# Weight splits skewed by a step between ScalarE and VectorE, and result banks handled one by one, in a two-layer decoder trunk on one core

## The chip, the cores and the metric

The kernel runs on 1 core of one Trainium2 chip. The metric is device time in microseconds (us) of one execution. The kernel before takes 1994.87 us (median of 3 runs, 1994.66 to 1995.28). In the traces the engines are named PE (TensorE, the matrix products), PEld (its weight loads), DVE (VectorE), ACT (ScalarE), POOL (GpSimdE) and SP (SyncE, which issues the DMA transfers).

## The reference

256 positions of 2048 channels go through two layers. Each layer adds to x a token mixer, a cross-attention to a memory of 256 positions, and a gated FFN, each behind an RMS norm. Only the structure matters here:

```python
def swiglu(h, w_in, w_out):
    g, u = jnp.split(h @ w_in, 2, axis=-1)
    return (jax.nn.silu(g) * u) @ w_out

for i in range(DEPTH):                       # DEPTH = 2
    h = rms_norm(x, norm_mix[i])
    if i % 2 == 0:
        x = x + pool_mixer(h, pool_w[ia], pool_scale[ia])
    else:
        x = x + dsa_attention(h, attn_w_in[ib], attn_w_out[ib], cos_a, sin_a, cos_i, sin_i)
    x = x + memory_cross_attention(rms_norm(x, norm_xattn[i]), memn,
                                   xattn_w_q[i], xattn_w_kv[i], xattn_w_o[i])
    x = x + swiglu(rms_norm(x, norm_ffn[i]), ffn_w_in[i], ffn_w_out[i])
return rms_norm(x, norm_final)
```

Everything is in float32. The FFN's hidden width is 5632; its weights are most of the 368 MB that are read.

## The kernel before

x stays in SBUF. The weights come once from HBM, as **pieces** of 128 x 2048 float32, in the order in which they are used. SP issues a transfer (L157, `load_to`) into one of three buffers named `raw`. Each piece is then **split** into two fp32r tiles: the high part, a copy on ScalarE (`high`, L167, tile `wh`), and the low part, raw minus high, on VectorE (`low`, L170, tile `wl`). The activations are split in the same way. A product of float32 accuracy is three products of fp32r, xh·wh, xh·wl and xl·wh: L413 to L415 outside the FFN (L438, L439 in the transposed form), L759 to L761 in the FFN (`three`). One such product is 128 x 128 by 128 x 512.

Some pieces of the FFN are of another kind, called "seven" here: they enter a scheme of seven instead of eight block products. Their split makes `bh`, `bl` from the piece itself, sums on VectorE within the piece (L200, L202, L203), and `th`, `tl` from the sums. Their left sides are the `sums` tiles: differences of blocks of the activations (`combine`, L402 to L405 on VectorE), which are split like the rest, the high by ScalarE, the low by VectorE.

The order of all instructions is that in which the Python code writes them; every engine takes its own in this order. The code of the products calls `hook` after each small group of them (in the FFN six products). `hook` runs a due job, a piece of side work, and one or two steps of the split of a coming piece (`split_unit`). A step of a plain piece is one half: high and low of 1024 columns. How far ahead the split may run is limited by the number of `w` tiles held: at most 8 exist, and `state["cap"]` limits the hooks to 6 (`W_SHORT`) or 8 (`W_BUFS`). Before the last use `w_get` does what is still missing. `split_unit` also calls for the load of the piece three ahead.

The cross-attention ends with the output product: four column blocks n of 512. After each, `done` adds the two banks to x (`add_to_x`, L506 on VectorE), and starts the next norm's work on that block: a square on ScalarE (L336), transposes on TensorE (L386), their high on ScalarE (L377), their low on VectorE (L379), and for the sums a scaled copy on ScalarE (L393).

The FFN runs over groups of hidden blocks, (0,4), (4,8), (8,11). `chunk_in` (22 calls in the kernel) multiplies 8 pieces into four banks; then VectorE adds the other parts of the result (L852), ScalarE takes Silu (L854), VectorE multiplies (L855). `chunk_out` (two halves n per group) multiplies the gated blocks by the second weights into four banks, and adds to x in the middle (`mid`, L895 to L902) and at the end (L912). `blocks` holds the products of both; it returns after the last of them, so that the code behind the loop handles the four banks in a row. There are four banks for such results, so that the next `blocks` needs the first of them at its first product.

## Time and profile before

| | |
|---|---|
| median of 3 runs | 1994.87 us (1994.66 to 1995.28) |
| profiled execution, its own time | 1993.54 us |
| its span | 1991.7 us |
| TensorE busy | 1953.1 us, 98% of the span |
| VectorE busy | 1554.7 us, 78% |
| ScalarE busy | 1024.1 us, 51% |
| transfers by SP's queue | 370.52 MB, 50.3% of 16 engines' span |
| mean granted TensorE clock | 0.994 of 2.4 GHz |

The terms of the sum come from one profiled execution. Its own time is 1.84 us more than its span and 1.33 us below the median. In time the kernel goes: start, memory keys and values and the first mixer to about 96 us; cross-attention to 192.75; the first FFN to 917; the sparse attention to 1206; cross-attention to 1257; the second FFN to 1981; final norm and output.

A row of a timeline gives the start and the length of an instruction, and in brackets how long the engine stood idle before it and which instruction released it. Rows that follow directly can be grouped, with a count. The products are pipelined: one shows some 0.39 us, but the next starts before it ends.

### The profile page before, as it was taken

How to read it: one execution, taken by the hardware profiler on the slowest of the kernel's cores; microseconds unless marked ns; L12 is line 12 of the kernel's file. 1: busy time of each engine (PE TensorE's matmuls, PEld its weight loads, DVE VectorE, ACT ScalarE, POOL GpSimd, SP SyncE). 2: the span in 40 equal slices, each digit the busy share in tenths (PEclk: the TensorE clock that was granted, in tenths of full speed). 3: DMA queues.
4: the chain of work that ended last, by engine and by line, in shares of the span. 5: the costliest groups of instructions: out<-in, count | busy, mean ns of one | idle time of the engine just before them, and what ended most of it. 6: DMA issues, size and time to landing. Idle time of an engine off the chain costs nothing.

```text
span 1991.7 us, 23621 instructions
## 1 busy us (share of the span) xinstructions
PE 1953.1 (98%) x8986; PEld 1617.5 (81%) x8986; DVE 1554.7 (78%) x2229; ACT 1024.1 (51%) x1462; POOL 29.0 (1%) x73
## 2 busy tenths in 40 slices
PE   9999999999999999999999999899999999999997
PEld 7887788888888888888788888688888888888886
DVE  7865778888888788897687665778878788887897
ACT  6655545455455544555445554655544455544553
POOL 0100000000000000001000000000000000000000
PEclk9999999999999999999999999999999999999999
DMA  9444544545554545545444453455545555544552
GB/s 375 168 150 169 189 171 170 210 186 218 204 195 169 204 177 212 210 169 174 178 149 148 148 193 125 153 208 210 211 169 190 190 192 217 204 191 182 187 204 105
DMA packets 53682, 372.08 MB, mean 187 GB/s; under 512 B 6336, under 2 KB 6976, under 8 KB 9536
## 3 DMA queue, kind: packets, MB, share of 16 engines
q1 hardware_dynamic: 53424, 370.52, 50.3%
q8 instruction: 70, 1.15, 0.2%
q14 instruction: 44, 0.36, 0.1%
q10 hardware_dynamic: 144, 0.05, 0.0%
HBM read 368.45 MB, written 2.10 MB: 186 GB/s over the span
## 4 chain that ended last, share of the span: by engine, by line
PE 91%; DVE 5%; ACT 2%; DMA 1%; issue 1%; SPq 0%; ACTq 0%; DVEq 0%
PE acc L759 19%; PE acc L761 19%; PE acc L760 19%; PE acc L415 5%; PE acc L413 5%; PE acc L414 5%; DVE wl L170 2%; PE acc L438 2%; PE sm L761 1%; PE tp L761 1%; PE tp L760 1%; PE sm L760 1%; PE sm L759 1%; PE tp L759 1%; PE acc L439 1%; DMA raw<-in_xk 1%
## 5 line engine op out<-in xcount | busy, mean ns | idle before, releaser
L170 DVE TENSOR_TENSOR wl<-raw,wh 128x1024 fp32r<-128x1024 f32 (+2 forms) x566 | 665.2, 1213 | 140.7 <-ACT wh L167 138.2
L167 ACT ACTIVATE wh<-raw 128x1024 fp32r<-128x1024 f32 (+2 forms) x566 | 567.1, 1045 | 261.4 <-PE acc L760 96.3
L759 PE MATMUL acc<-wh,big 128*128 128x512 f32 x1616 | 636.5, 394 | 18.5 <-DVE x L506 12.3
L761 PE MATMUL acc<-wh,big 128*128 128x512 f32 x1616 | 630.9, 390 | 0.0
L760 PE MATMUL acc<-wl,big 128*128 128x512 f32 x1616 | 630.6, 390 | 0.0
L759 PEld LDWEIGHTS acc<-wh,big 128*128 128x128 f32 x1616 | 304.5, 188 | 84.4 <-DVE x L506 13.2
L761 PEld LDWEIGHTS acc<-wh,big 128*128 128x128 f32 x1616 | 304.3, 188 | 63.8
L760 PEld LDWEIGHTS acc<-wl,big 128*128 128x128 f32 x1616 | 304.7, 189 | 61.8
L167 ACT ACTIVATE th<-raw 128x1024 fp32r<-128x1024 f32 x186 | 132.4, 766 | 168.7 <-DVE raw L200 129.6
L413 PE MATMUL acc<-wh,big 128*128 128x512 f32 (+1 forms) x480 | 200.6, 418 | 0.0
L415 PE MATMUL acc<-wh,big 128*128 128x512 f32 (+1 forms) x480 | 185.7, 387 | 0.0
L414 PE MATMUL acc<-wl,big 128*128 128x512 f32 (+1 forms) x480 | 184.9, 385 | 0.0
L170 DVE TENSOR_TENSOR bl<-raw,bh 128x1024 fp32r<-128x1024 f32 x124 | 113.1, 954 | 74.9 <-ACT bh L167 74.6
L167 ACT ACTIVATE bh<-raw 128x1024 fp32r<-128x1024 f32 x124 | 98.0, 838 | 128.7 <-issue 79.3
L170 DVE TENSOR_TENSOR tl<-raw,th 128x1024 fp32r<-128x1024 f32 x186 | 151.3, 863 | 5.6 <-ACT th L167 5.6
L415 PEld LDWEIGHTS acc<-wh,big 128*128 128x128 f32 x480 | 90.0, 188 | 18.7
L414 PEld LDWEIGHTS acc<-wl,big 128*128 128x128 f32 x480 | 90.6, 189 | 16.6 <-issue 1.9
L413 PEld LDWEIGHTS acc<-wh,big 128*128 128x128 f32 x480 | 90.3, 188 | 16.4 <-issue 1.9
L438 PE MATMUL acc<-big,wh 128*128 128x512 f32 x256 | 97.0, 417 | 3.2 <-DVE big L379 2.4
L371 DVE TENSOR_TENSOR big<-tp,big 128x512 fp32r<-128x512 f32 x44 | 30.4, 691 | 59.3 <-ACT big L370 59.3
L200 DVE TENSOR_TENSOR raw<-raw 128x1024 f32<-128x1024 f32 x62 | 75.5, 1218 | 0.0
L439 PE MATMUL acc<-big,wl 128*128 128x256 f32 x256 | 72.6, 283 | 1.0 <-DVE wl L170 1.0
(212 smaller groups left out, 2056.5 us busy)
## 6 DMA issues: line engine op xcount, KB each, us to landing
raw<-in_fi SPq DMA_DIRECT2D x176, 1024.0 KB, 4.8
raw<-in_fo SPq DMA_DIRECT2D x88, 1024.0 KB, 4.8
raw<-in_wq SPq DMA_DIRECT2D x16, 1024.0 KB, 4.9
raw<-in_wao SPq DMA_DIRECT2D x16, 1024.0 KB, 4.9
raw<-in_xv SPq DMA_DIRECT2D x8, 1024.0 KB, 6.0
raw<-in_xq SPq DMA_DIRECT2D x8, 1024.0 KB, 4.8
raw<-in_xo SPq DMA_DIRECT2D x8, 1024.0 KB, 4.8
raw<-in_wqi SPq DMA_DIRECT2D x8, 1024.0 KB, 4.9
```

What stands on the lines that cost most here:

```text
L167: A.activation(dst, src, AF.Copy)
L170: V.tensor_tensor(dst, src, hi.bitcast(F32), op=ALU.subtract)
L200: V.tensor_tensor(r[:, 1:3, :], r[:, 1:4:2, :], r[:, 2:3, :].to_broadcast([P, 2, 512]), op=ALU.add)
L371: V.tensor_tensor(dst_l, src, dst_h.bitcast(F32), op=ALU.subtract)
L413: T.matmul(acc[:, :w], lhsT=xh, rhs=wh[:, c0:c0 + w], start=first, stop=False)
L414: T.matmul(acc[:, :w], lhsT=xh, rhs=wl[:, c0:c0 + w], start=False, stop=False)
L415: T.matmul(acc[:, :w], lhsT=xl, rhs=wh[:, c0:c0 + w], start=False, stop=last)
L438: T.matmul(acc, lhsT=wh[:, c0:c0 + P], rhs=xt[:, k, :], start=first, stop=False)
L439: T.matmul(acc[:, S:2 * S], lhsT=wl[:, c0:c0 + P], rhs=xt[:, k, 0:S], start=False, stop=last)
L759: T.matmul(acc, lhsT=xh, rhs=wh, start=first, stop=False)
L760: T.matmul(acc, lhsT=xh, rhs=wl, start=False, stop=False)
L761: T.matmul(acc, lhsT=xl, rhs=wh, start=False, stop=last)
```

## The change

Three edits.

First, the split is skewed. `split_unit` writes the ScalarE part of one step and then the VectorE part of the step before it, which waits in `owed`. The load of the piece three ahead is issued when the last VectorE part of a piece is written. The steps of a "seven" piece are cut anew: bh/bl with the first add (L200, in the new file L204), the other adds, the inner half of th/tl, the outer quarters.

Second, `blocks` takes a function `done(f, t, acc)` that it calls when the last product of one bank is written, instead of handing back all four banks after the last one. In `chunk_in` that function adds, and takes the Silu or the gated product; in `chunk_out` it adds to x.

Third, the line that raised the limit from 6 to 8 tiles in the last output product of the cross-attention is gone; the limit is raised where the FFN begins its groups.

```diff
@@ -171,63 +171,82 @@
 
     def split_plain(i, t, w):
 
+        n = UNIT if i else 512
+
         def unit(c, first):
-            def fn():
+            def act():
                 if first:
                     parts[i] = (w_tile("wh"), w_tile("wl"))
-                wh, wl = parts[i]
-                high(wh[:, c], t[:, c])
-                low(wl[:, c], t[:, c], wh[:, c])
-            return 2 if first else 0, fn
-        n = UNIT if i else 512
+                high(parts[i][0][:, c], t[:, c])
+
+            def dve():
+                low(parts[i][1][:, c], t[:, c], parts[i][0][:, c])
+
+            return 2 if first else 0, act, dve
...
+
+        def a0():
             p["bh"], p["bl"] = w_tile("bh"), w_tile("bl")
             parts[i] = p
-            for c in (slice(0, 1024), slice(1536, 2048)):
+            for c in own:
                 high(p["bh"][:, c], t[:, c])
+
+        def d0():
+
+            for c in own:
                 low(p["bl"][:, c], t[:, c], p["bh"][:, c])
-
-        def s1():
-
-            p["th"], p["tl"] = w_tile("th"), w_tile("tl")
...
+
+        def d1():
             V.tensor_tensor(r[:, 3, :], r[:, 1, :], r[:, 3, :], op=ALU.add)
             V.tensor_tensor(r[:, 0, :], r[:, 3, :], r[:, 0, :], op=ALU.add)
 
-        def s2():
-            for c in (slice(1536, 2048), slice(0, 512)):
+        def a2():
+            p["th"], p["tl"] = w_tile("th"), w_tile("tl")
+            high(p["th"][:, 512:1536], t[:, 512:1536])
+
+        def d2():
+            low(p["tl"][:, 512:1536], t[:, 512:1536], p["th"][:, 512:1536])
+
+        def a3():
+            for c in outer:
                 high(p["th"][:, c], t[:, c])
-            low(p["tl"][:, 512:1536], t[:, 512:1536], p["th"][:, 512:1536])
-
-        def s3():
-            for c in (slice(1536, 2048), slice(0, 512)):
+
+        def d3():
+            for c in outer:
                 low(p["tl"][:, c], t[:, c], p["th"][:, c])
 
-        return [(2, s0), (2, s1), (0, s2), (0, s3)]
+        return [(2, a0, d0), (0, None, d1), (2, a2, d2), (0, a3, d3)]
 
     def split_unit(must=False):
 
-        i = state["split"]
-        if i >= len(pieces):
-            return
-        load_to(i + RAW_BUFS)
-        if not steps:
-            steps.extend(split_seven(i, raws[i][0]) if pieces[i][2] else split_plain(i, *raws[i]))
-        if state["held"] + steps[0][0] > (W_BUFS if must else state["cap"]):
-            assert not must
-            return
-        steps.popleft()[1]()
-        if not steps:
-            raws.pop(i)
-            state["split"] += 1
+        i = state["begun"]
+        if not steps and i < len(pieces):
+            load_to(i + 1)
+            new = split_seven(i, raws[i][0]) if pieces[i][2] else split_plain(i, *raws[i])
+            steps.extend((n, act, dve, i if j == len(new) - 1 else None) for j, (n, act, dve) in enumerate(new))
+            state["begun"] += 1
+        dve = end = None
+        if steps and state["held"] + steps[0][0] <= (W_BUFS if must else state["cap"]):
+            _, act, dve, end = steps.popleft()
+            if act is not None:
+                act()
+        assert owed or dve is not None or not must
+        if owed:
+            fn, of = owed.popleft()
+            fn()
+            if of is not None:
+                raws.pop(of)
+                state["split"] += 1
+                load_to(of + 1 + RAW_BUFS)
+        if dve is not None:
+            owed.append((dve, end))
 
     def w_get(key, ahead=0):
         i = state["cur"] + ahead
@@ -733,8 +752,6 @@
             add_to_x(acc, n)
             w_done()
             nxt.chunk(n)
-            if n == 2:
-                state["cap"] = W_BUFS
             hook()
...
-        def blocks(keys, operand, mid, t_major=0):
+        def blocks(keys, operand, mid, done, t_major=0):
 
 
             acc = [acc_tile() for _ in range(4)]
@@ -775,6 +792,8 @@
                     ws = c(((1, 2), (0, 3))[u][f])
                     three(acc[2 * t + f], xt[:, k0 + u, t * P:(t + 1) * P], xt[:, k0 + u, S + t * P:S + (t + 1) * P],
                           w[0][:, ws], w[1][:, ws], i == 0 and u == 0, i == len(keys) - 1 and u == 1)
+                if i == len(keys) - 1:
+                    done(f, t, acc[2 * t + f])
 
             def eight(i, w):
                 for f, t in ((0, 0), (0, 1), (1, 0), (1, 1)):
@@ -822,9 +841,6 @@
                     w = w_get(keys[i], i - n)
                     for f in range(2):
                         plain(i, w, f, t)
-                yield t, acc
-            if not t_major:
-                yield None, acc
...
-            (_, acc), = blocks([("fi", L, j, kp) for kp in pairs], operand, mid)
-            r = xn.get_rstd()
-            c11, c12, c21, c22 = part
-            for i, y in ((0, c11), (2, c21), (1, c12), (3, c22)):
-                V.tensor_tensor(y, acc[i], y, op=ALU.add)
-            for t, (g, h) in enumerate(((c11, c12), (c21, c22))):
-                A.activation(g, g, AF.Silu, scale=r[:, t:t + 1])
-                V.scalar_tensor_tensor(h, h, r[:, t:t + 1], g, op0=ALU.mult, op1=ALU.mult)
-            h = (c12, c22)
+            def done(f, t, acc):
+
+                y = part[2 * t + f]
+                V.tensor_tensor(y, acc, y, op=ALU.add)
+                r = xn.get_rstd()[:, t:t + 1]
+                if f == 0:
+                    A.activation(y, y, AF.Silu, scale=r)
+                else:
+                    V.scalar_tensor_tensor(y, y, r, part[2 * t], op0=ALU.mult, op1=ALU.mult)
+
+            blocks([("fi", L, j, kp) for kp in pairs], operand, mid, done)
+            h = (part[1], part[3])
...
             end = last and n == 1 and isinstance(nxt, Final)
-            for t, acc in blocks([("fo", L, n, kp) for kp in range(2 * t0, 2 * t1)], operand, mid, 3 if end else 0):
-                for i, (f, u) in enumerate(((0, 0), (1, 0), (0, 1), (1, 1)) if t is None else ((0, t), (1, t))):
-                    V.tensor_tensor(xc(f, u), acc[2 * u + f], xc(f, u), op=ALU.add)
-                    if t is not None:
-                        nxt.half(2 * n + f, u)
+            def done(f, t, acc):
+                V.tensor_tensor(xc(f, t), acc, xc(f, t), op=ALU.add)
+                if end:
+                    nxt.half(2 * n + f, t)
+
+            blocks([("fo", L, n, kp) for kp in range(2 * t0, 2 * t1)], operand, mid, done, 3 if end else 0)
             if end:
```

The file grows, so lines move: L506 becomes L525, L379 L398, L402 to L405 become L421 to L424, L852 and L855 become L867 and L872, L895 to L902 become L914 to L921, L912 becomes L930; L167 and L170 keep their numbers.

VectorE at the end of the first cross-attention's output product, where the last two adds to x (L506, in the new file L525, a pair each for n = 2 and n = 3) stand among the lows of the weights (L170) and of the transposed activations (L379, L398). Before:

```order
L379 SCALAR_TENSOR_TENSOR big<-tp,gains,big 128x256 x2
L506 TENSOR_TENSOR x<-acc,x 128x512 x2
L379 SCALAR_TENSOR_TENSOR big<-tp,gains,big 128x256 x2
L170 TENSOR_TENSOR wl<-raw,wh 128x1024 x2
L379 SCALAR_TENSOR_TENSOR big<-tp,gains,big 128x256 x2
L170 TENSOR_TENSOR wl<-raw,wh 128x1024
L379 SCALAR_TENSOR_TENSOR big<-tp,gains,big 128x256 x2
L170 TENSOR_TENSOR wl<-raw,wh 128x1024
L506 TENSOR_TENSOR x<-acc,x 128x512 x2
L170 TENSOR_TENSOR wl<-raw,wh 128x1024 x2
```

Now:

```order
L525 TENSOR_TENSOR x<-acc,x 128x512 x2
L398 SCALAR_TENSOR_TENSOR big<-tp,gains,big 128x256 x2
L170 TENSOR_TENSOR wl<-raw,wh 128x1024
L398 SCALAR_TENSOR_TENSOR big<-tp,gains,big 128x256 x2
L170 TENSOR_TENSOR wl<-raw,wh 128x1024
L398 SCALAR_TENSOR_TENSOR big<-tp,gains,big 128x256 x2
L525 TENSOR_TENSOR x<-acc,x 128x512 x2
L170 TENSOR_TENSOR wl<-raw,wh 128x1024 x4
L170 TENSOR_TENSOR bl<-raw,bh 128x1024
```

Between the two pairs of adds stood three pairs of L379 and four plain lows. Now the three pairs of L398 stand there as before, but only two plain lows; the last pair of adds stands ahead of the other four.

VectorE a little later, at the sums of that FFN (the two combines L402 to L405, the low halves `sums`, the plain lows `wl`). Before:

```order
L402 TENSOR_TENSOR tmp<-tmp 128x128
L403 TENSOR_TENSOR tmp<-tmp 128x128
L404 TENSOR_TENSOR tmp<-tmp 128x128
L405 TENSOR_TENSOR tmp<-tmp 128x128
L170 TENSOR_TENSOR wl<-raw,wh 128x1024
L170 TENSOR_TENSOR sums<-tmp,sums 128x512
L170 TENSOR_TENSOR wl<-raw,wh 128x1024
L170 TENSOR_TENSOR sums<-tmp,sums 128x512
L170 TENSOR_TENSOR wl<-raw,wh 128x1024 x4
```

Now:

```order
L421 TENSOR_TENSOR tmp<-tmp 128x128
L422 TENSOR_TENSOR tmp<-tmp 128x128
L423 TENSOR_TENSOR tmp<-tmp 128x128
L424 TENSOR_TENSOR tmp<-tmp 128x128
L170 TENSOR_TENSOR sums<-tmp,sums 128x512
L170 TENSOR_TENSOR wl<-raw,wh 128x1024
L170 TENSOR_TENSOR sums<-tmp,sums 128x512
L170 TENSOR_TENSOR wl<-raw,wh 128x1024 x4
```

The first low of the sums moved ahead of a plain low; both are a place nearer to the combine.

VectorE at the end of the first block that goes back into x (the last of the eight adds in the middle, the plain lows, the four adds L912, in the new file L930, and the next piece's bl). Before:

```order
L898 TENSOR_TENSOR x<-sm,x 128x512
L899 TENSOR_TENSOR x<-x,tmp 128x512
L902 TENSOR_TENSOR x<-x,tmp 128x512
L170 TENSOR_TENSOR wl<-raw,wh 128x1024 x4
L912 TENSOR_TENSOR x<-acc,x 128x512 x4
L170 TENSOR_TENSOR bl<-raw,bh 128x1024
L170 TENSOR_TENSOR bl<-raw,bh 128x512
L200 TENSOR_TENSOR raw<-raw 128x1024
```

Now:

```order
L917 TENSOR_TENSOR x<-sm,x 128x512
L918 TENSOR_TENSOR x<-x,tmp 128x512
L921 TENSOR_TENSOR x<-x,tmp 128x512
L170 TENSOR_TENSOR wl<-raw,wh 128x1024 x3
L930 TENSOR_TENSOR x<-acc,x 128x512
L170 TENSOR_TENSOR wl<-raw,wh 128x1024
L930 TENSOR_TENSOR x<-acc,x 128x512
L170 TENSOR_TENSOR wl<-raw,wh 128x1024
L930 TENSOR_TENSOR x<-acc,x 128x512 x2
L170 TENSOR_TENSOR bl<-raw,bh 128x1024
L170 TENSOR_TENSOR bl<-raw,bh 128x512
L204 TENSOR_TENSOR raw<-raw 128x1024
```

The four adds, which stood together behind four lows, now stand behind three, and one low lies between the first and the second, and one between the second and the third.

## Rows read from the trace of the kernel before

**Rows 1.** The page: part 1 (busy us, share of the span, instructions, by engine) and part 4 (the chain that ended last, by engine).

```profile
PE 1953.1 (98%) x8986; PEld 1617.5 (81%) x8986; DVE 1554.7 (78%) x2229; ACT 1024.1 (51%) x1462; POOL 29.0 (1%) x73
...
PE 91%; DVE 5%; ACT 2%; DMA 1%; issue 1%; SPq 0%; ACTq 0%; DVEq 0%
```

**Rows 2.** The waits of TensorE over the whole span: what waited, for what, us in total, times, longest us.

```profile
PE acc L759 <- DVE x L506: 12.3, 2, 6.2
PE acc L759 <- DVE x L912: 5.3, 8, 0.8
PE acc L761 <- DVE sums L170: 3.0, 2, 1.5
...
PE acc L759 <- ACT bh L167: 0.9, 1, 0.9
```

**Rows 3.** Busy time by stretch. Columns: the stretch in us, its length, busy time and instructions of PE, PEld, DVE, ACT and POOL, the granted TensorE clock (1.00 is 2.4 GHz), the share of the DMA, GB/s.

```profile
200.00:206.60 6.60, 4.79 (x11) 3.80 (x12) 4.62 (x5) 1.79 (x2) 0.00 (x0) 0.50 0.54 185
...
226.30:232.00 5.70, 5.70 (x25) 4.70 (x26) 5.70 (x6) 3.40 (x4) 0.00 (x0) 1.00 0.66 207
...
29.20:32.50 3.30, 3.30 (x12) 2.81 (x11) 3.30 (x8) 3.27 (x8) 0.00 (x0) 0.50 1.04 428
```

**Rows 4.** The timeline of VectorE (DVE) around the first products of the first FFN. Columns: start us, us, engine, line, operation, out<-in, tile, count, and in brackets the idle time before it and what ended that.

```profile
192.22 2.36 DVE L170 TENSOR_TENSOR wl<-raw,wh 128x1024 fp32r<-128x1024 f32 x2 [2.46 <-ACT wh L167]
...
195.46 1.23 DVE L170 TENSOR_TENSOR wl<-raw,wh 128x1024 fp32r<-128x1024 f32 x1
196.60 0.87 DVE L379 SCALAR_TENSOR_TENSOR big<-tp,gains,big 128x256 fp32r<-128x256 f32 x2
199.93 1.22 DVE L170 TENSOR_TENSOR wl<-raw,wh 128x1024 fp32r<-128x1024 f32 x1 [2.46 <-ACT wh L167]
201.07 1.28 DVE L506 TENSOR_TENSOR x<-acc,x 128x512 f32<-128x512 f32 x2
```

**Rows 5.** The timeline of ScalarE (ACT) in the same place.

```profile
193.03 0.83 ACT L377 ACTIVATE big<-tp,gains 128x256 fp32r<-128x256 f32 x2
...
195.30 0.85 ACT L377 ACTIVATE big<-tp,gains 128x256 fp32r<-128x256 f32 x2
197.51 0.84 ACT L393 ACTIVATE tmp<-tp,gains 128x256 f32<-128x256 f32 x2 [1.35 <-DVE big L379]
...
198.85 2.94 ACT L167 ACTIVATE wh<-raw 128x1024 fp32r<-128x1024 f32 x3
```

**Rows 6.** The timeline of TensorE (PE) in the same place.

```profile
195.02 0.39 PE L760 MATMUL acc<-wl,big 128*128 128x512 f32 x1
195.25 0.39 PE L761 MATMUL acc<-wh,big 128*128 128x512 f32 x1
201.81 0.80 PE L759 MATMUL acc<-wh,big 128*128 128x512 f32 x1 [6.17 <-DVE x L506]
...
206.65 0.39 PE L761 MATMUL acc<-wh,big 128*128 128x512 f32 x1
```

**Rows 7.** The timeline before the second group of products with the sums in the first FFN, first VectorE, then TensorE.

```profile
214.33 0.88 DVE L379 SCALAR_TENSOR_TENSOR big<-tp,gains,big 128x256 fp32r<-128x256 f32 x2 [0.95 <-ACT big L377]
...
217.71 1.22 DVE L170 TENSOR_TENSOR tl<-raw,th 128x1024 fp32r<-128x1024 f32 x1
...
222.46 0.29 DVE L405 TENSOR_TENSOR tmp<-tmp 128x128 f32<-128x128 f32 x1
224.40 1.23 DVE L170 TENSOR_TENSOR wl<-raw,wh 128x1024 fp32r<-128x1024 f32 x1 [1.65 <-ACT wh L167]
...
224.42 0.39 PE L760 MATMUL acc<-bl,sums 128*128 128x512 f32 x1
226.28 0.50 PE L761 MATMUL acc<-bh,sums 128*128 128x512 f32 x1 [1.47 <-DVE sums L170]
```

**Rows 8.** The timeline at the first end of a block that goes back into x, first VectorE, then TensorE.

```profile
458.10 4.62 DVE L170 TENSOR_TENSOR wl<-raw,wh 128x1024 fp32r<-128x1024 f32 x4
462.64 2.48 DVE L912 TENSOR_TENSOR x<-acc,x 128x512 f32<-128x512 f32 x4
...
462.35 0.39 PE L761 MATMUL acc<-wh,big 128*128 128x512 f32 x1
463.47 0.47 PE L759 MATMUL acc<-wh,big 128*128 128x512 f32 x1 [0.73 <-DVE x L912]
463.78 0.39 PE L760 MATMUL acc<-wl,big 128*128 128x512 f32 x1
```

**Rows 9.** The same at the fifth such end, before the last group of the first FFN.

```profile
881.82 1.82 DVE L170 TENSOR_TENSOR bl<-raw,bh 128x1024 fp32r<-128x1024 f32 x2
...
885.95 1.22 DVE L200 TENSOR_TENSOR raw<-raw 128x1024 f32<-128x1024 f32 x1
887.20 0.69 DVE L202 TENSOR_TENSOR raw<-raw 128x512 f32<-128x512 f32 x1
...
884.39 0.47 PE L759 MATMUL acc<-wh,big 128*128 128x512 f32 x1 [0.55 <-DVE x L912]
```

**Rows 10.** The timeline of TensorE in the start, its longest wait there.

```profile
28.07 0.50 PE L438 MATMUL acc<-big,wh 128*128 128x512 f32 x1 [1.86 <-DVE big L379]
```

**Rows 11.** Groups of instructions by line and operation. Columns: line, engine, operation, out<-in, shape, count | busy us, mean ns | idle us before, by releaser. First TensorE, then ScalarE (L854 is the Silu).

```profile
L760 PE MATMUL acc<-wl,big 128*128 128x512 f32 x1616 | 630.6, 390 | 0.0
...
L854 ACT ACTIVATE tmp<-tmp,rs 128x512 f32<-128x512 f32 x44 | 29.5, 717 | 41.4 <-DVE tmp L852 41.4
```

More of the change, by code (lines that the diff above doesn't have):

```diff
@@ L137, in trunk_kernel @@
                     plan(("fo", L, n, kp), a["fo"][L, n, kp], kp in SEVEN_OUT)
-    state = {"load": 0, "split": 0, "cur": 0, "hook": 0, "held": 0, "cap": W_SHORT}
-    raws, parts, steps = {}, {}, deque()
+    state = {"load": 0, "split": 0, "cur": 0, "hook": 0, "held": 0, "cap": W_SHORT, "begun": 0}
+    raws, parts, steps, owed = {}, {}, deque(), deque()
     UNIT = 1024
@@ L188, in split_seven @@
         p = {}
-        def s0():
+        own, outer = (slice(0, 1024), slice(1536, 2048)), (slice(1536, 2048), slice(0, 512))
+        def a0():
             p["bh"], p["bl"] = w_tile("bh"), w_tile("bl")
             parts[i] = p
-            for c in (slice(0, 1024), slice(1536, 2048)):
+            for c in own:
                 high(p["bh"][:, c], t[:, c])
+        def d0():
+            for c in own:
                 low(p["bl"][:, c], t[:, c], p["bh"][:, c])
-        def s1():
-            p["th"], p["tl"] = w_tile("th"), w_tile("tl")
@@ L200, in s1 @@
             V.tensor_tensor(r[:, 1:3, :], r[:, 1:4:2, :], r[:, 2:3, :].to_broadcast([P, 2, 512]), op=ALU.add)
-            high(p["th"][:, 512:1536], t[:, 512:1536])
+        def d1():
             V.tensor_tensor(r[:, 3, :], r[:, 1, :], r[:, 3, :], op=ALU.add)
             V.tensor_tensor(r[:, 0, :], r[:, 3, :], r[:, 0, :], op=ALU.add)
-        def s2():
-            for c in (slice(1536, 2048), slice(0, 512)):
+        def a2():
+            p["th"], p["tl"] = w_tile("th"), w_tile("tl")
+            high(p["th"][:, 512:1536], t[:, 512:1536])
```

## The prediction

> **What bounds the kernel now.** I read the page first: TensorE is busy for 98% of the span, VectorE for 78%, and the chain that ended last is 91% TensorE and 5% VectorE [rows 1]. The reader is to see that a cheaper split by itself gives nothing: the chain runs through the products, and only the places where TensorE stands still can be won. So the waits of TensorE come next [rows 2]. Three kinds make up most of them: two waits of 6.2 us for the add of an output block into x at L506, eight of at most 0.8 us for the adds at L912 (with one of 0.9 us put down to ScalarE's bh, of the same kind by its place in the program), and two of 1.5 us for the low half of the "sums". The third view is the granted clock by stretches [rows 3]: right after the 6.2 us wait TensorE runs for 6.6 us at 0.50, that is at 1.2 GHz, and then at 2.4 GHz again. After a wait of 1.5 us the clock stays at 1.00. The last view is the timeline around one place of each kind, which gives the durations below.
>
> Products that follow each other without a wait start 0.23 us apart (195.02 to 195.25 [rows 6]). A wait costs more than its idle time, so I count from start to start.
>
> **First products of each FFN.** The products stop after the start at 195.25 and go on at 201.81: 6.56 us instead of 0.23, so 6.33 us are lost. From 201.81 to 206.65 eleven steps take 4.84 us instead of 11 x 0.227 = 2.50, so the low clock costs 2.34 us more [rows 6]. Together 8.67 us; [rows 2] shows two such waits, one for each FFN, so 17.3 us.
> The bank that TensorE waits for is freed by L506, and in the trace its two adds stand last on VectorE: behind pairs of L379 (which need ScalarE's L377), and behind a low at 199.93, which waited 2.46 us for a high [rows 4]. That high was late because ScalarE stood at L393 until 197.51, waiting 1.35 us for L379, and began the high at 198.85, after that pair and a square [rows 5]. VectorE's new order has those two adds before the low. I walk it with the durations of the trace. ScalarE's two highs end at 193.03, and L377 takes 0.83 for a pair [rows 5]. On VectorE the low that starts at 192.22 alone ends at about 193.4 (half of 2.36 us); the pair of L379 behind it ends at about 194.3; the next low, 1.23 us, at 195.45; the pair behind that needs ScalarE's second pair of L377 (done about 195.1 now: two pairs and the square between them, without the high that ends at 195.4 in the trace) and ends near 196.3; the first L506 (0.64 us, half of 1.28) ends at about 196.9 [rows 4]. With a little for the semaphore TensorE goes on between 196.95 and 197.5; I take 197.2. What stays is 197.2 - 195.48 = 1.7 us, with the slow first step 1.8. If the clock holds, each start saves 8.67 - 1.8 = 6.9 us, both 13.7 us.
> Does it hold? The 1.47 us wait before 226.28 was followed by 1.00; the 1.86 us wait before 28.07 by 3.3 us at 0.50 [rows 3, 7, 10]. The new wait lies between these two. Between ends that near I go by what TensorE did before: ahead of 226 us it worked without a break, as it does ahead of 195 us, while ahead of 28 us the start's waits lie. So I take 1.00, and keep the other for the range. The bound is what the trace shows after the longest wait: 2.34 us each.
>
> **The low half of the sums.** The product at 226.28 starts 1.86 us after the one at 224.42: 1.63 us lost, twice, 3.3 us [rows 7]. VectorE had finished combining the sums at 222.75, stood 1.65 us for a high, did that low (1.23 us), and only then the low of the sums. In the new order the sums' low stands directly behind the combine, and the plain low comes after it. But TensorE comes earlier too, by the 6.9 us of the step above: it wants the low at 224.65 - 6.9 = 217.7. The last pair of L379 ahead of the combine (214.33 to 215.2) hangs on transposes behind TensorE's restart and moves by the same 6.9 us, to 208.3. The three adds of the split that follow it in the trace now stand before it, so what is left is the stretch from the tl low at 217.71 to the end of the combine, 5.0 us, then ScalarE's high of the sums and its low, 0.6 to 0.7 us each: about 214.7. A margin of 3 us is left, so I take the full 3.3 us; the bound is 0.
>
> **Bank adds one by one.** At 458.10 VectorE does four lows (4.62 us) and reaches the four L912 only at 462.64, when the products end: TensorE waits 0.73 us, counted from start to start 463.47 - 462.35 - 0.23 = 0.89, and another 0.08 in the step to 463.78 [rows 8]; so 0.24 more than the idle time. The new order has the first add behind three lows, and one low less before the eight adds of the middle. It ends between 458.1 - 1.15 + 3 x 1.15 + 0.64 = 461.0 and, if the middle cannot move ahead, 462.2; TensorE comes at 462.58. Each later add has a low ahead of it (1.15 + 0.64 = 1.8 us) and comes due a bank later (six products, 1.37 us), so from the middle of the two ends (461.6, margin 1) the second has 0.6 and the third 0.2 us left; the fourth follows at once. Eight regular ends: 5.3 - 0.55 + 0.88 = 5.63 us of idle time [rows 2, 9], and 8 x 0.24 = 1.9: 7.5 us.
> One end is different: at 884.39 the split is further ahead, and the steps of a "seven" piece fall between the adds. Its new order is: first add, two bl lows, the L200 add, second add, two more adds of the split, third and fourth add. The bl lows (1.82 us), L200 (1.22 us) and two adds of 0.69 us [rows 9] now stand between the adds of the banks, and the second bank comes free about 1.05 us after TensorE wants it, the third 0.64 us: 1.7 us instead of 0.55. So 1.2 us are lost, and this term comes to 6.3 us. In the first half of each FFN (gates and their products) TensorE waits for no add at the ends before; the new order puts a low behind each of two adds (1.8 us for the two against 1.37 us a bank), and a bank is wanted again only three banks (4.1 us) after its last product, so about 3 us are left. At the last of them the bl lows and L200 (3.0 us) stand between the adds and use that up. I take 0, and 1 us for each of the two FFNs as its bound.
>
> **The skew elsewhere, and the limit.** A low is issued one hook later, which is about 1.4 us (six products). Not one of the 1616 products L760, the first to need a low, waits in the trace [rows 11]; what hides the delay is the pieces that are split ahead, up to the limit of tiles. If that cover were gone it would cost up to 1.4 us at a piece and show as waits of L760 on wl. The load of the piece three ahead is issued with a piece's last low; no wait of TensorE in the FFNs is on a transfer [rows 2], so 0. At the start the DMA is full (share 1.04 at 29 to 32 us [rows 3]) and small operations change places around the restart at 28.07 [rows 10]. I take 0, with the half of 3.3 us that the low clock cost there, 1.7 us, to either side. The six-tile limit lasts longer, and changes only how far the split runs ahead at the FFN start; its effect is in the walk. The end of the program keeps its order: 0.
>
> **Sum.** 13.7 + 3.3 + 6.3 = 23.3 us off the profiled run's 1993.54 (span 1991.7 and 1.84 around it): 1970.2. The median of the runs is 1.33 above the profiled one: 1971.6 us.
>
> **Rivals.**
> *The wait at the FFN starts stays longer and the clock falls.* If ScalarE still has a high (2.94 us for three [rows 5]) and its wait of 1.35 us ahead of what the adds need, TensorE goes on near 199.5, and the clock falls as at 201.81. Cost: 2 x 2.34 for the clock alone, 1976.3; with the later restart 2 x 4.6, 1980.8. For it: the 28.07 row. Against it: the 226.28 row.
> The Trainium skill, "TensorE: Matmul & The Clock Gate", section "A second HAM failure mode: psum-queue depth-cycling", says that frequent short pauses while a kernel cycles through banks make the clock swing between its levels. By that rule the short ends of rows 8 would each cost a slow stretch too, and their removal would give up to 8 x 2.3 = 18 us more, about 1953. The trace does not agree: the step from 463.47 to 463.78 is 0.31 us, not the 0.44 of the slow stretch (4.84 / 11), so I give this 2 in 100.
> *The sums' wait stays,* because TensorE comes earlier by as much as the chain that feeds it: 1971.6 + 3.3 = 1974.9.
> *Only the short ends go.* The two long waits have another last cause than VectorE's order (a ScalarE operation that the walk puts too early): 1994.9 - 6.3 = 1988.6. Against it: for the adds at 201.07 the trace names no releaser, they only had their turn [rows 4].
> *VectorE holds up the splits: slower than before.* An add or a gated product now stands in VectorE's row before the lows of the next piece, and waits there for TensorE's bank or for ScalarE's Silu. A Silu (0.72 us [rows 11]) can stand behind a high (about 1 us [rows 5]): 1.7 us in which VectorE does nothing. With 22 ends of gated blocks (44 Silus, two each) that is 37 us if nothing is hidden, 1971.6 + 37 = 2009. It decides at the point where the delay is larger than the lead of the lows over their products; the trace shows only that this lead is nowhere used up [rows 11]. For it: VectorE is busy for 78% of the span, and there is little room at an end. Against it: 22% is 437 us, and between a bank's add and its gated product the new order has an add and two lows.
> On this the Trainium skill, "TensorE: Matmul & The Clock Gate", section "Architectural detail: the array is 16× 32×32, not 1× 128×128", says that ScalarE's and VectorE's queues are strictly first in, first out. The trace agrees (L506 at 201.07 behind a low that waited 2.46 us), and it speaks against putting waiting adds among the lows.
>
> **Chances.** The forecast 0.62, with its own range 1968 to 1975; the sums stay 0.10; the clock falls or a longer wait 0.13; short ends alone 0.07; the clock bonus 0.02; slower by held-up splits 0.06. About 0.2% (4 us) can be told from no change. The range 1966 to 1982 leaves out the short ends alone, the bonus, the slower case and the tails. Faster by over 0.2%: 0.91, counting 0.02 of the short ends as no change; within 0.2%: 0.04, with the part of the slower case that cancels the gain; slower: 0.05.
>
> **What would show it.** Right: no wait of 6 us before the first products of an FFN, under 2 us in its place and clock 1.00 behind it; no wait of L761 on the sums; waits on the bank adds at one place only, that of 884.39. Wrong: waits of L760 on wl in the FFNs, a clock of 0.50 after 197, VectorE idle at the gated products with TensorE waiting for a bank, or a span above 1975 with none of these.

## The result and the profile after

The changed kernel takes 1970.28 us (median of 4 runs, 1968.48 to 1970.77) against 1995.07 us before: a ratio of 0.9874, 95% interval 0.9857 to 0.9891. The forecast was 1971.6 us. The profiled execution took 1970.56 us, its span is 1968.8 us, 22.9 us shorter than before.

First the page, parts 1 and 4, which answer to [rows 1]:

```profile
PE 1946.9 (99%) x8986; PEld 1617.6 (82%) x8986; DVE 1554.8 (79%) x2229; ACT 1026.8 (52%) x1462; POOL 31.6 (2%) x73
...
PE 95%; DVE 2%; ACT 1%; DMA 1%; issue 0%; SPq 0%; ACTq 0%; DVEq 0%
```

No engine has less to do: 8986 products as before, VectorE's busy time equal to 0.1 us. VectorE's share of the chain that ended last fell from 5% to 2%, and TensorE's rose from 91% to 95%. What went is waiting, and the view of TensorE's waits shows which (compare [rows 2]):

```profile
PE acc L776 <- DVE x L930: 2.8, 1, 2.8
...
PE acc L776 <- DVE x L525: 1.9, 2, 0.9
```

The two waits of 6.2 us are two of 0.9 us. The sums' waits are gone, and of the nine waits on the bank adds one is left, which has grown from 0.55 [rows 9] to 2.8 us.

**The first products of the first FFN**: VectorE, ScalarE and TensorE, as in [rows 4 to 6].

```profile
191.50 1.23 DVE L170 TENSOR_TENSOR wl<-raw,wh 128x1024 fp32r<-128x1024 f32 x1 [2.46 <-ACT wh L167]
...
193.97 1.21 DVE L170 TENSOR_TENSOR wl<-raw,wh 128x1024 fp32r<-128x1024 f32 x1
195.10 0.87 DVE L398 SCALAR_TENSOR_TENSOR big<-tp,gains,big 128x256 fp32r<-128x256 f32 x2
195.89 1.28 DVE L525 TENSOR_TENSOR x<-acc,x 128x512 f32<-128x512 f32 x2
...
193.64 0.85 ACT L396 ACTIVATE big<-tp,gains 128x256 fp32r<-128x256 f32 x2
...
195.31 0.39 PE L778 MATMUL acc<-wh,big 128*128 128x512 f32 x1
196.63 0.50 PE L776 MATMUL acc<-wh,big 128*128 128x512 f32 x1 [0.93 <-DVE x L525]
196.97 0.40 PE L777 MATMUL acc<-wl,big 128*128 128x512 f32 x1
```

And the stretch behind the wait (columns as in [rows 3]):

```profile
196.70:203.00 6.30, 6.30 (x28) 5.18 (x29) 5.03 (x6) 6.01 (x9) 0.00 (x0) 1.00 0.54 190
```

The adds to x begin at 195.89 instead of 201.07, and ScalarE's second pair of L396 at 193.64 instead of 195.30. From 195.31 to 196.97 two steps take 1.66 us instead of 0.46: 1.2 us lost instead of 8.67. The steps after it are 0.23 us long, and the granted clock is 1.00.

**The sums and a regular block end**, as in [rows 7] and [rows 8].

```profile
213.84 0.69 DVE L170 TENSOR_TENSOR sums<-tmp,sums 128x512 fp32r<-128x512 f32 x1
...
217.25 0.39 PE L778 MATMUL acc<-bh,sums 128*128 128x512 f32 x1
```

```profile
447.97 3.49 DVE L170 TENSOR_TENSOR wl<-raw,wh 128x1024 fp32r<-128x1024 f32 x3
451.38 0.68 DVE L930 TENSOR_TENSOR x<-acc,x 128x512 f32<-128x512 f32 x1
...
453.37 0.39 PE L776 MATMUL acc<-wh,big 128*128 128x512 f32 x1
```

The sums' low ends at 214.5, 2.7 us before the product that reads it. The first bank add ends at 452.1, and TensorE writes that bank again at 453.37, without a wait.

**The fifth block end**, where the wait grew ([rows 9]): SP, ScalarE, VectorE, TensorE, then the windows of the stretch (columns as in [rows 3]).

```profile
864.96 0.33 SPq L157 DMA_DIRECT2D raw<-in_fo  x1
...
870.01 1.58 ACT L167 ACTIVATE bh<-raw 128x1024 fp32r<-128x1024 f32 x2 [5.74 <-DMA raw<-in_fo]
...
863.66 5.76 DVE L170 TENSOR_TENSOR wl<-raw,wh 128x1024 fp32r<-128x1024 f32 x5
869.34 0.69 DVE L930 TENSOR_TENSOR x<-acc,x 128x512 f32<-128x512 f32 x1
871.10 1.83 DVE L170 TENSOR_TENSOR bl<-raw,bh 128x1024 fp32r<-128x1024 f32 x2 [1.07 <-ACT bh L167]
872.84 1.22 DVE L204 TENSOR_TENSOR raw<-raw 128x1024 f32<-128x1024 f32 x1
873.98 0.69 DVE L930 TENSOR_TENSOR x<-acc,x 128x512 f32<-128x512 f32 x1
...
871.55 0.39 PE L778 MATMUL acc<-wh,big 128*128 128x512 f32 x1
874.72 0.79 PE L776 MATMUL acc<-wh,big 128*128 128x512 f32 x1 [2.79 <-DVE x L930]
...
877.96 0.47 PE L776 MATMUL acc<-wh,big 128*128 128x512 f32 x1
```

```profile
874.80:878.00 3.20, 3.20 (x11) 2.51 (x11) 3.17 (x5) 1.70 (x3) 0.00 (x0) 0.54 0.04 15
```

The reader is to follow it backwards. TensorE waits for the second bank add. That stands behind bl and L204; bl waits 1.07 us for ScalarE's bh; bh waits for a transfer; and the transfer was issued at 864.96, when the first of the lows at 863.66 had freed its buffer. That low stands behind the eight adds of the middle. The wait is followed by a stretch at half the clock.

### The profile page after: what moved, and what is told of

It is laid out like the page before. It is cut to its first block, busy times and chain, and to the rows that moved or that the text cites. A ratio compares the mean times of both kernels' runs of the same rounds, so it can differ in the third digit from the quotient of the medians.

```text
span 1968.8 us, 23586 instructions
## 1 busy us (share of the span) xinstructions
PE 1946.9 (99%) x8986; PEld 1617.6 (82%) x8986; DVE 1554.8 (79%) x2229; ACT 1026.8 (52%) x1462; POOL 31.6 (2%) x73
## 4 chain that ended last, share of the span: by engine, by line
PE 95%; DVE 2%; ACT 1%; DMA 1%; issue 0%; SPq 0%; ACTq 0%; DVEq 0%
PE acc L776 20%; PE acc L778 20%; PE acc L777 20%; PE acc L434 5%; PE acc L432 5%; PE acc L433 5%; PE acc L457 2%; PE tp L778 1%; PE tp L777 1%; PE tp L776 1%; PE sm L777 1%; PE sm L776 1%; PE sm L778 1%; PE acc L458 1%; DMA raw<-in_xk 1%; PE tp L885 1%
## 5 line engine op out<-in xcount | busy, mean ns | idle before, releaser
L170 DVE TENSOR_TENSOR wl<-raw,wh 128x1024 fp32r<-128x1024 f32 (+2 forms) x566 | 665.4, 1210 | 110.4 <-ACT wh L167 108.8
L167 ACT ACTIVATE wh<-raw 128x1024 fp32r<-128x1024 f32 (+2 forms) x566 | 569.1, 1045 | 286.0 <-issue 106.1
L777 PE MATMUL acc<-wl,big 128*128 128x512 f32 x1616 | 629.5, 390 | 0.0
L777 PEld LDWEIGHTS acc<-wl,big 128*128 128x128 f32 x1616 | 303.9, 188 | 61.5
L167 ACT ACTIVATE th<-raw 128x1024 fp32r<-128x1024 f32 x186 | 132.4, 765 | 103.4 <-DVE raw L204 99.9
L167 ACT ACTIVATE bh<-raw 128x1024 fp32r<-128x1024 f32 x124 | 98.0, 838 | 156.6 <-issue 93.7
L170 DVE TENSOR_TENSOR bl<-raw,bh 128x1024 fp32r<-128x1024 f32 x124 | 113.0, 953 | 84.3 <-ACT bh L167 84.3
L170 DVE TENSOR_TENSOR tl<-raw,th 128x1024 fp32r<-128x1024 f32 x186 | 151.2, 862 | 0.0
L389 ACT ACTIVATE big<-tp 128x512 fp32r<-128x512 f32 x44 | 26.3, 599 | 100.1 <-PE tp L885 100.1
L204 DVE TENSOR_TENSOR raw<-raw 128x1024 f32<-128x1024 f32 x62 | 75.6, 1219 | 0.0
```

The costliest lines, as they stand in the source:

```text
L167: A.activation(dst, src, AF.Copy)
L170: V.tensor_tensor(dst, src, hi.bitcast(F32), op=ALU.subtract)
L204: V.tensor_tensor(r[:, 1:3, :], r[:, 1:4:2, :], r[:, 2:3, :].to_broadcast([P, 2, 512]), op=ALU.add)
L389: A.activation(dst_h, src, AF.Copy)
L777: T.matmul(acc, lhsT=xh, rhs=wl, start=False, stop=False)
```

## Experiments

The theory after the result: three causes that have little to do with each other. The FFN starts are freed by VectorE's order at one place, the block ends by the adds among the lows, the sums by the skew; and the skew also makes the wait at the fifth end, through the transfer. The rivals: the skew alone carries the gain; or the edits simply add up.

**One edit alone.** The skew:

```diff
-        steps.popleft()[1]()
...
+            _, act, dve, end = steps.popleft()
+            if act is not None:
+                act()
...
+            fn, of = owed.popleft()
+            fn()
...
+            owed.append((dve, end))
```

> The kernel before with the skewed split only; banks handled after the last product and the limit raised at n = 2 as before. Theory: at an FFN start a third plain low still stands ahead of the last adds to x, but its high is now issued a step earlier, so TensorE goes on near 199 instead of 201.8, and the clock may still fall; some 3 us saved at each start. The two waits on the sums vanish (3.3 us). The eight ends at the adds L912 keep their waits. About 9.5 us in all, 1985.5 us. Rival, the skew carries the whole gain of the FFN starts: 1977 or less. Rival, the skew gives nothing by itself: 1995.

The banks:

```diff
+                if i == len(keys) - 1:
+                    done(f, t, acc[2 * t + f])
```

> The kernel before with each bank handled with its own last products only. Theory: the waits on the adds at the ends of the blocks into x go at all nine places, since without the skew no low slips behind the adds of the middle; 7.5 to 8.5 us, about 1987. The 6.2 us waits and the sums' waits stay. Rival, the order of the lows is needed too for these waits to go: 1993 to 1995.

The limit:

```diff
-            if n == 2:
-                state["cap"] = W_BUFS
```

> The kernel before with the six-tile limit kept until the FFN only, one line. Theory: no plain low stands between the last pair of transposed lows and the last adds to x any more, which is all that the 6.2 us wait was; the adds come near 196.1 to 196.9 as in the changed kernel, the clock stays at 1.00, 7.3 us at each start, about 1980.3. The sums' waits of 1.5 us stay, because the plain low ahead of the sums' low is still there. Rival, the skew is what frees the adds: 1994 to 1995. Rival, with fewer tiles split ahead TensorE waits for lows at the first pieces instead: above 1985 with waits of L760.

| kernel | median, us | ratio to before (95%) |
|---|---|---|
| before, beside these three and the next | 1993.85 | |
| skew alone | 1991.37 | 0.9989 (0.9980 to 0.9998) |
| banks alone | 1990.16 | 0.9980 (0.9970 to 0.9989) |
| limit alone | 1979.93 | 0.9927 (0.9911 to 0.9944) |

The limit alone came out as expected, and it is the largest part: 14 us for two lines. VectorE at the FFN start of that kernel, TensorE behind it, and its waits:

```profile
192.72 2.36 DVE L170 TENSOR_TENSOR wl<-raw,wh 128x1024 fp32r<-128x1024 f32 x2 [2.46 <-ACT wh L167]
195.00 1.66 DVE L379 SCALAR_TENSOR_TENSOR big<-tp,gains,big 128x256 fp32r<-128x256 f32 x4
196.57 1.28 DVE L506 TENSOR_TENSOR x<-acc,x 128x512 f32<-128x512 f32 x2
...
197.31 0.50 PE L757 MATMUL acc<-wh,big 128*128 128x512 f32 x1 [1.17 <-DVE x L506]
```

```profile
PE acc L757 <- DVE x L910: 5.8, 9, 0.8
PE acc L759 <- DVE sums L170: 2.9, 2, 1.5
```

With six tiles the split does not begin another piece there. The two lows that start at 195.46 and 199.93 in [rows 4] no longer stand ahead of the adds, and with the second goes its wait of 2.46 us for a high. The other two kinds of wait stay.

The skew alone was expected at 1985.5 and came 6 us later. Its FFN starts wait 2.4 us, as the expectation said (a low still stands ahead of the adds, its high issued earlier), and the sums' waits went. What was not foreseen are the block ends:

```profile
PE acc L778 <- DVE x L931: 15.1, 10, 5.6
PE acc L778 <- DVE x L525: 4.9, 2, 2.4
```

Five lows instead of four stand between the adds of the middle and those of the end. At the fifth end bl stood ahead of the adds before, too ([rows 9]); now L204, L207 and L208 do as well, and bl itself waits 1.6 us for its high: 5.6 us there, 15.1 in all against 6.2 [rows 2]. Two gated blocks wait for their adds as well, 0.6 us each.

The banks alone were expected at 1987 and took 1990.2. Of the nine waits at the block ends seven went; one of 0.2 us and the 0.5 us at the fifth end, where bl still stands ahead of the adds, stayed. And the first gated block of each FFN got a new wait of 0.9 us, because its adds stand behind a low that waits for a high (VectorE of that kernel):

```profile
247.59 1.22 DVE L170 TENSOR_TENSOR wl<-raw,wh 128x1024 fp32r<-128x1024 f32 x1 [3.08 <-ACT wh L167]
248.73 1.28 DVE L850 TENSOR_TENSOR tmp<-acc,tmp 128x512 f32<-128x512 f32 x2
```

**One edit left out.** Each kernel here is the changed one with one of the three diffs above taken back.

> The changed kernel with the old split order: banks one by one and the limit, no skew. Theory: everything but the sums' waits goes, and the 2.8 us wait of the changed kernel near 875 is not there, because it comes from a low that the skew puts behind the eight adds of the middle, so that a raw buffer and its transfer come late. 14.7 + 8.3 = 23 us, about 1972, with two waits of 1.5 us on the sums and none at the fifth block end. Rival, the wait near 875 comes from the banks handled one by one and stays: 1976 or more.

> The changed kernel with the banks handled after the last product as before: skew and limit. From the run of the skew alone (1991.4), less what the limit adds at the FFN starts (its waits there fall from 2.4 to 0.9 us and no clock is lost): 1.5 to 2.8 us each. Theory: 1985 to 1989, with waits near 1 us at eight block ends and 5.6 us with a slow stretch at the fifth. Rival, the three edits add up: 1994 - 14 - 3 = 1977.

> The changed kernel without the limit: skew and banks one by one, the limit raised at n = 2 as before. Theory: the FFN starts are those of the skew alone (2.4 us waits, 1.5 us more each than with the limit, and 1.7 us for the clock where it falls), everything else is that of the changed kernel: 1973 to 1977. So the limit is worth 3 to 6 us on top of the skew and the banks, against 14 alone. Rival, the edits add up and the limit is worth its 14 us here too: 1984.

| kernel | median, us | before beside it | ratio (95%) |
|---|---|---|---|
| without the skew | 1975.48 | 1993.85 | 0.9906 (0.9892 to 0.9921) |
| without the banks | 1986.84 | 1993.61 | 0.9967 (0.9955 to 0.9979) |
| without the limit | 1974.89 | 1994.32 | 0.9907 (0.9892 to 0.9921) |
| changed, beside the second | 1970.22 | 1993.61 | 0.9883 (0.9868 to 0.9897) |
| changed, beside the third | 1970.25 | 1994.32 | 0.9879 (0.9862 to 0.9895) |

The edits don't add up. Skew and banks give 2.5 and 3.7 us alone, but 19.4 together (without the limit): the banks take away the long waits that the skew makes at the block ends, and the skew gives the adds lows whose highs are done. The limit is worth 14 us alone and 4.6 us on top of the other two, since the skew by itself shortens the FFN starts from 6.2 to 2.4 us. Two of the three expectations held. Without the skew 1972 was expected; the wait at the fifth end is 0.5 us there, as before the change, so the growth to 2.8 us does belong to the skew. But the 0.9 us waits of the banks alone are there too, and a wait of 2.9 us at the start:

```profile
PE acc L757 <- DVE tmp L848: 1.8, 2, 0.9
...
PE acc L757 <- DVE x L911: 0.5, 1, 0.5
```

The 2.9 us belong to the restart of [rows 10] at some 29 us. With the old split order it was 1.9, 2.3, 1.0 and 2.9 us in four profiles, in kernels that don't differ there, so I read nothing from one of them.

**The wait at the fifth end.** First the changed kernel again, with an expectation of its own.

> The changed kernel itself once more, beside the others on one chip. Theory: 1968 to 1971 us, the one long wait near 875 us again at 2.8 us, because it hangs on a transfer whose start is set by VectorE's order and not by chance; its clock may stay at 1.00 behind it in some executions, which is worth 1.7 us. Rival, the wait is an accident of that one execution: no wait above 1 us at that place.

1970.22 us (1969.78 to 1970.61), with a wait of 2.7 us at 873.7 and the clock at half level for 3.4 us behind it; a third profile (below) has 2.8 us at 874.4. It is no accident. Then that low moved ahead of the middle, and with it only the start of the transfer:

```diff
                 v, u = tmp(), tmp()
+                if last and n == 0:
+                    settle()
                 A.activation(v, m[1], AF.Copy)
```

Here `settle` writes the one owed VectorE step and asks for the next load, as `split_unit` does.

> The changed kernel with the owed low written before the eight adds of the middle instead of behind them, in the first half of the last group only. Theory: that low frees the raw buffer, so the transfer starts some 5 us earlier and bh does not wait for a landing; what stays are the split's instructions between the bank adds, the 1.7 us that were forecast, so the wait falls from 2.8 to 1.4 to 1.8 us and the time by 1 us, or by 2.8 if the clock then holds. Rival, the landing is not the cause and the row of instructions alone makes 2.8: nothing changes there.

1967.87 us (1967.47 to 1968.81), 2.35 us under the changed kernel beside it. SP, ScalarE, VectorE, TensorE and the stretch behind the wait:

```profile
860.22 0.33 SPq L157 DMA_DIRECT2D raw<-in_fo  x1
...
866.02 1.58 ACT L167 ACTIVATE bh<-raw 128x1024 fp32r<-128x1024 f32 x2 [1.15 <-DMA raw<-in_fo]
...
870.43 1.81 DVE L170 TENSOR_TENSOR bl<-raw,bh 128x1024 fp32r<-128x1024 f32 x2
...
874.04 0.50 PE L780 MATMUL acc<-wh,big 128*128 128x512 f32 x1 [1.60 <-DVE x L936]
...
876.05 0.47 PE L780 MATMUL acc<-wh,big 128*128 128x512 f32 x1
```

```profile
874.10:878.00 3.90, 3.90 (x21) 3.15 (x22) 3.87 (x7) 3.17 (x7) 0.00 (x0) 1.00 0.03 13
```

The transfer is issued 4.7 us earlier, bl has no wait for bh any more, and the wait falls to 1.60 us, with the clock at 1.00 behind it. So the 2.8 us are two things: 1.6 us of instructions between two bank adds, and 1.1 to 1.2 us of a late landing. The clock's part can be read behind the wait: from the restart to the product after the next four transposes TensorE takes 877.96 - 874.72 = 3.24 us in the changed kernel and 876.05 - 874.04 = 2.01 us here, 1.2 us less. Landing and clock together make the 2.4 us.

This does not say yet why only the fifth end waits. At the eleventh, the same place in the second FFN, VectorE of the changed kernel has the same row (five lows, first add, bl, L204, second add), ScalarE's bh waits for a transfer there too (4.17 us), and TensorE waits for no add. VectorE of the changed kernel at the first add of the middle in each FFN, then at the eleventh end:

```profile
858.49 0.68 DVE L914 TENSOR_TENSOR tmp<-tp,tmp 128x512 f32<-128x512 f32 x1
...
1908.87 0.69 DVE L914 TENSOR_TENSOR tmp<-tp,tmp 128x512 f32<-128x512 f32 x1 [0.42 <-PE tp L778]
...
1921.04 0.69 DVE L930 TENSOR_TENSOR x<-acc,x 128x512 f32<-128x512 f32 x1 [1.23 <-PE acc L778]
1921.64 1.82 DVE L170 TENSOR_TENSOR bl<-raw,bh 128x1024 fp32r<-128x1024 f32 x2
...
1924.52 0.68 DVE L930 TENSOR_TENSOR x<-acc,x 128x512 f32<-128x512 f32 x1
```

In the second FFN VectorE is level with TensorE and waits for it at both adds. In the first it waits at neither: its L914 starts more than 4 us after the products that it reads, the last of which began at 853.9. Ahead of it stand 6 us of small instructions that prepare the tables of the sparse attention (L964 to L994, 848.93 to 855.17), and the second FFN has none. So the instructions between two adds cost TensorE time where VectorE is late already. No run takes that work away, so this part is argued and not shown.

Next, the hooks put off behind all four adds:

```diff
-                    if (f, t) != (1, 1):
+                    if (f, t) != (1, 1) and not (late and i == len(keys) - 1):
                         hook()
+                for _ in range(3 if late and i == len(keys) - 1 else 0):
+                    hook()
```

> The changed kernel with the three hooks of the last piece moved behind its four bank adds, at the fifth and eleventh block end only (first half of the last group). Theory: the adds stand behind one another again there and wait for no split; the 2.8 us wait and the slow stretch behind it go, 2.9 + 1.7 = 4.6 us off, 1964 to 1967 and some 4 us under the changed kernel. Rival, the split that is put off comes late for the next pieces and TensorE waits there instead: no gain, with waits on bl or bh after 880.

1968.75 us: 1.5 us instead of 4.6. The wait on the add went, and two others came:

```profile
878.44 0.63 PE L405 MATMUL tp<-ident,x 128*128 128x128 f32 x4 [1.73 <-DVE big L398]
...
1946.06 0.50 PE L777 MATMUL acc<-wl,big 128*128 128x512 f32 x1 [0.95 <-DVE wl L170]
```

The split that was put off stood ahead of the transposed activations, and in the second FFN a low came late. The rival of that expectation was right about the kind, but not about the tiles. Last, both moves in a gentler form, the low ahead of the middle and one hook put off, in the first FFN only:

```diff
-                    if (f, t) != (1, 1):
+                    if (f, t) != ((0, 0) if late and i == len(keys) - 1 else (1, 1)):
                         hook()
```

> The changed kernel, at the fifth block end with two moves: the owed low before the eight adds of the middle (as in the run before), and the hook between the first and the second bank put off to the fourth, so that the second add stands right behind the first, ahead of bl and L204. Theory: the remaining 1.6 us wait goes, the clock stays, and unlike with three hooks put off nothing comes late: 1.8 us under the run with the low alone (1967.9), 1965.5 to 1966.5, some 4 us under the changed kernel. Rival, the third or fourth bank waits instead (behind bl, L204, L207, L208) or the transposed activations come late as at 878: no gain over 1967.9.

> The changed kernel beside these two on the same chip: 1968.5 to 1971 us, the wait near 874 us again at 2.7 to 2.8 us.

1967.44 us (1966.79 to 1967.70) beside 1970.25 (1968.93 to 1970.73): 2.8 us under the changed kernel, with a ratio of 0.9866 (0.9851 to 0.9881) to before. That is the lowest median here, but it can't be told from the low alone (0.9872, 0.9857 to 0.9886). It gained some 1 us less than expected. The 1.6 us wait became 0.51, now on the third bank, with 0.36 us for the transposed activations behind it at 877.80, as its rival had it in part:

```profile
873.95 0.47 PE L780 MATMUL acc<-wh,big 128*128 128x512 f32 x1 [0.51 <-DVE x L936]
```

## Why the prediction came out as it did

The time was right within 1.3 us, and the terms were too, with one exception. "Measured" is the time between the same two products of TensorE in the trace before and in the trace after:

| term | forecast | measured |
|---|---|---|
| FFN starts | 13.7 | 7.45 + 7.34 = 14.8 |
| sums | 3.3 | 1.8 + 1.8 = 3.6 |
| eight regular block ends | 7.5 | 7.8 |
| fifth block end | -1.2 | -3.2 |
| sum | 23.3 | 23.0; the span is 22.9 shorter |

By its rows the fifth end is 874.72 - 871.55 - 0.23 = 2.9 us now, and some 1.3 us for the slow steps; before it was 0.8. That the sum is so near is in part luck: the fifth end took 2.0 us more than forecast, and the other three terms gave 1.7 us more. For the profiled execution the sum said 1970.2 us, and it took 1970.56. The 1.3 us between 1971.6 and 1970.28 come from the 1.33 us that were added for the median; the changed kernel's median lies 0.28 us below its profiled execution instead.

*FFN starts.* The walk had the order of the lows and transposed lows right, put the add's end at 196.9 where it was 196.5, and rightly forecast full clock behind the wait. It was 0.6 us a start too long, for two reasons. It started VectorE's row with the low at 192.22, as in the trace before, and in the changed kernel that low starts at 191.50; after a wait of 0.46 us for ScalarE behind it, 0.4 us were left of that. And it gave TensorE 0.3 us after the add's end, where the trace before shows 0.1 (201.71 to 201.81) and the one after as well (196.53 to 196.63). Its first paragraph has TensorE run for 6.6 us at half clock; that window of [rows 3] begins during the wait, and the term rightly uses the 4.84 us of the products. What the walk did not say is which edit clears the place. The prediction gave the six-tile limit half a sentence ("its effect is in the walk"). Limit alone and the kernel without it show that it clears the place by itself, and that the skew clears part of it.

*Sums.* Forecast 214.7 for the end of their low and 217.7 for TensorE; measured 214.5 and 217.25.

*Block ends.* The margin of the first add was forecast as 1 us and is 1.3 (452.06 to 453.37). The step that failed is the fifth end. There the prediction counted bl, L204 and two adds between the bank adds and got a wait of 1.7 us; it measured 2.8. The run with the early low measures 1.6 us for the part that was counted. Missing was the transfer: the prediction said of the loads "no wait of TensorE in the FFNs is on a transfer, so 0". That view names only the engine that came last, and here the transfer is two engines back. The prediction's reason why this end is different, the steps of a "seven" piece between the adds, holds at the eleventh end too, which does not wait. Behind the longer wait the clock fell as well, which the prediction had priced at the wrong place, the FFN start.

*Skew elsewhere.* No L777 waits for a low in the FFNs, so the delay of a hook is covered, as said.

*Rivals.* The slower one did not come: no wait on a gated product and no late low. But its mechanism, an add that waits in VectorE's row behind something else, is what the banks alone show at 248.73, and what decides the fifth end. The clock rival did not come, but its question was hardly put: the wait came out shorter (0.93 us) than both rows that the prediction weighed (1.47 and 1.86 us). In later runs the clock stayed behind waits of 1.60 and 1.73 us, which lie between those rows, and went either way behind 2.43 us (last section). "Only the short ends go" and "the sums stay" are out by the waits. The larger bonus from the clock at the short ends is out too: their removal brought 7.8 us, about what their idle time and restart were worth (7.5).

## What to carry to other kernels

Where one in-order engine both frees result banks and prepares later operands, look for the instruction ahead of the release that waits for a third engine; a limit on how far the preparation runs ahead can remove it with one line. Don't judge such edits one at a time: two that gave 2.5 and 3.7 us here gave 19 together, since each made waits that the other took away. And follow a delayed release one step further than the engine that waits: a low that slips behind other work also holds the buffer for the next transfer.

## What the runs showed of the hardware

Whether the clock falls after a wait of some 2.4 us was not settled by its length. In two kernels with the same two waits of 2.43 us at the FFN starts it fell at one of them, a different one in each. The skew alone, at 197.88 and 1264.35, then the kernel without the limit, at 197.73 and 1253.94 (columns as in [rows 3]):

```profile
198.60:201.90 3.30, 3.30 (x10) 2.52 (x9) 3.30 (x3) 1.81 (x2) 0.00 (x0) 0.50 0.49 122
...
1264.50:1270.00 5.50, 5.50 (x25) 4.54 (x26) 5.36 (x6) 3.97 (x5) 0.00 (x0) 1.00 0.69 243
```

```profile
198.60:201.90 3.30, 3.30 (x16) 2.74 (x15) 3.30 (x4) 3.01 (x4) 0.00 (x0) 1.00 0.43 119
...
1254.70:1257.90 3.20, 3.20 (x9) 2.42 (x9) 3.20 (x3) 1.77 (x2) 0.00 (x0) 0.50 0.41 110
```

The same 3.3 us hold 10 products in one and 16 in the other. Behind the waits of 0.9 to 1.7 us in the FFNs of these runs the clock stayed at 1.00; behind those of 2.7 to 2.9 us it fell in all four profiles that have one. And in the skew alone it fell while TensorE was still waiting, as this stretch inside the 5.6 us wait shows:

```profile
881.30:884.80 3.50, 0.00 (x0) 0.00 (x0) 3.43 (x6) 2.02 (x3) 0.00 (x0) 0.50 0.51 213
```
